# Where a residual block is turned: DMA transposes and TensorE transposes exchanged at two places, and joins written into spent space

## The chip, the cores and the metric

The kernel runs on one core of a Trainium2 chip. The metric is device time in microseconds (us), the median of several runs; less is better. The engines of the core are named as in the profile: PE is TensorE (PEld its weight loads), DVE is VectorE, ACT is ScalarE, POOL is GpSimd, SP is SyncE, which here only issues DMAs.

## The reference

One block of a hybrid streaming encoder, in float32, with 256 rows of 2048 columns. Cut to what matters here:

```python
h      = rmsnorm(x, g_mix);  proj = h @ w_in            # q,k,v twice, and two gates
merged = sigmoid(gate_sb) * (y_sb @ w_sb_out) + sigmoid(gate_ca) * (y_ca @ w_ca_out)
x      = x + merged @ w_mix_out
h      = rmsnorm(x, g_ffn);  g_ff, u_ff = split(h @ w_ffn_in)
x      = x + (silu(g_ff) * u_ff) @ w_ffn_out
h      = rmsnorm(x, g_ple)
x      = x + sigmoid(h @ w_ple_gate) * (p @ w_ple_in)   # the last gate
out    = rmsnorm(x, g_final)
```

`y_sb` is a stick-breaking attention and `y_ca` a chunked attention with a relative bias; neither is touched by the change.

## The kernel before

**Products.** Each float32 operand is split into a rounded high part and the remainder (`hi`, `lo`); a product is the sum of three TensorE products (`three`, L313). Activations lie in tables `T1`, `T2`, `T3`, transposed: a table holds, for each 128 columns of the activation (a `kt`, 16 of them for 2048 columns), a high and a low part of 128 x 256. A block is 512 columns, four `kt`. Weights are streamed from HBM in pieces of 128 x 1024 (`raw`, L244, issued on SP), cast on ACT (`hi`, L283, L298, L301) and subtracted on DVE (`lo`, L260). There are five `raw` buffers, one or two more in the later stages, and three or four pairs of `hi` and `lo`; casts run up to three pieces ahead of the products.

**Units.** Most products run in units of two blocks of output columns and all `kt`. In a unit some pairs of `kt` are pair pieces: seven products in place of eight, with sums of weights (`xf`, made on DVE and cast at L304) and sums of activations (`forms`, made by `sums_of` or `pair_sums`). The pair pieces add into four PSUM banks of their own (`su`), taken from the pool of banks that the unit before used for its results; `mid` (L883) copies them into the tile `C` (four planes of 128 x 512), and the unit's end adds `C` to the results. The mixer's two output projections (`w_sb_out`, `w_ca_out`) are not units: they are plain groups of four pieces for each block of 512 columns.

**Turning a block.** When a block of activations is ready, it must be transposed into a table. There are two ways.

`into_table` (L481) does eight 128 x 128 transposes on TensorE (L490) into PSUM; `table_part` then writes the high part on ACT and the low part on DVE from PSUM, times the gain of the norm where there is one (L543 and L544), and for `kt` whose pair is among `forms` it makes their sums.

`by_dma` (L497) takes the float32 words apart into 16-bit halves on ACT (`turn`, L506, two copies into `planes`), issues one DMA transpose of both planes on SP (L507, into `turned`), and later joins the halves again on ACT (`join`, L512, two copies of 128 x 1024 halves, one for each two `kt`) into a tile `af`, from which `table_part` goes on. The tag `af` has two buffers in the late stages; the joins, the squares of the norms (L125), `pair_sums` and the tile `fm` of `sums_of` all draw on it:

```python
af = state["work"]("af").rearrange("p (k s) -> p k s", k=2)
with tc.issue_after(state["cast"].ins):
    nc.scalar.copy(af.bitcast(U16).rearrange("p k (s h) -> p h k s", h=2), halves[:, :, k0 : k0 + 2, :])
table_part(dst, 4 * c + k0, af, gain, forms, pairs, af)
```

`at` gives how many pieces after the block the turn and the first join are put into the program; the second join follows one piece later.

**Who uses which.** `out_post` (L958) multiplies the mixer's projections by their gates, adds the two, and turns each of the four blocks (key `mg`, into `T1`) by `into_table`. `next_tables` (L1004) runs at the end of a unit for both of its blocks: after the mixer's last projection (key `ffn`, into `T3`) all four blocks go by DMA; after the last feed-forward projection (key `ple`, into `T1`) blocks 0 and 1 go by DMA and 2 and 3 by `into_table`. `hidden` (L1088) turns the feed-forward's hidden blocks, all but one by DMA.

**Order.** Work between pieces stands in two lists: `tasks`, one run after each piece (`later` puts three empty ones ahead), all of them before the first pair piece of a unit takes its banks; and `asides`, with the piece at which each is due. Within that, each engine's instructions are laid out by a planner, from a model of the timeline; `issue_after` holds an instruction behind another. SP issues the weight loads and the DMA transposes in one queue, in order.

Of the kernel before, what the change touches and what calls it, by code (L numbers as in the profile page):

```python
# [9 lines left out]
F32 = mybir.dt.float32  # L10
F32R = mybir.dt.float32r
U16 = mybir.dt.uint16
# [5 lines left out]
P = 128  # L18
S = 256
NT = 2  # L20
# [12 lines left out]
NB = 512  # L33
# [3 lines left out]
PAIRS = (2, 4, 6)  # L37
MIX_PAIRS = (4, 6)
# [15 lines left out]
def block_kernel(ctx: ExitStack, tc: tile.TileContext, x, p, w_in, w_sb_out, w_ca_out, w_mix_out,  # L54
# [19 lines left out]
    dma_w = nc.sync  # L74
# [12 lines left out]
    def aux(name):  # L87
        pool, width, tag = ps_ax[-1]
        return pool.tile([P, width], F32, tag=tag, name=name)
# [8 lines left out]
    T1 = bp.tile([P, KD, 2, S], F32R, tag="T1", name="T1")  # L98
    T2 = bp.tile([P, KD, 2, S], F32R, tag="T2", name="T2")
    x_ = bp.tile([P, NT, D], F32, tag="x", name="x")  # L100
# [306 lines left out]
    state = dict(loaded=0, split=0, at=0, raw=0, hl=0, ext=0, ps=ps_mm, fourth=None, ring=0, places=0, hold=False)  # L407
    late = dict(ps=[ps_mm])
# [27 lines left out]
    def later(fn, n=3):  # L436

        for _ in range(n):
            tasks.append((None, lambda: None))
        tasks.append((None, fn))  # L440
# [40 lines left out]
    def into_table(dst, c, src, gain=None, key=None, forms=None, pool=None, pairs=PAIRS):  # L481


        n = ps_ax[-1][1] // S if pool is None else 2
        for k0 in range(0, 4, n):
            ps = (aux("tp") if pool is None else late["ps"][pool].tile([P, 512], F32, tag="mm", name="tp"))
            ps = ps.rearrange("p (k s) -> p k s", k=n)
            for k in range(n):
                for t in range(NT):
                    nc.tensor.transpose(ps[:, k, t * P : (t + 1) * P], src[:, t, (k0 + k) * P : (k0 + k + 1) * P], ident)  # L490
            step = n if forms is None else 2
            for k1 in range(0, n, step):
                table_part(dst, 4 * c + k0 + k1, ps[:, k1 : k1 + step, :], gain, forms, pairs)
        for k in range(4):
            done.add((key, 4 * c + k))

    def by_dma(dst, c, src, planes, turned, key, at, gain=None, forms=None, pairs=PAIRS):  # L497

        words = src.bitcast(U16).rearrange("p t (k n h) -> p t h k n", h=2, n=P)
        planes, turned = (v.rearrange("p t n -> p (t n)").bitcast(U16) for v in (planes, turned))  # L500
        split = planes.rearrange("p (h k t n) -> p t h k n", h=2, k=4, t=NT)
        halves = turned.rearrange("p (h k s) -> p h k s", h=2, k=4)

        def turn():
            for t in range(NT):
                nc.scalar.copy(split[:, t], words[:, t])  # L506
            dma_w.dma_start_transpose(turned.rearrange("p (j s) -> p j s", s=P), planes)  # L507

        def join(k0):
            af = state["work"]("af").rearrange("p (k s) -> p k s", k=2)  # L510
            with tc.issue_after(state["cast"].ins):
                nc.scalar.copy(af.bitcast(U16).rearrange("p k (s h) -> p h k s", h=2), halves[:, :, k0 : k0 + 2, :])  # L512
            table_part(dst, 4 * c + k0, af, gain, forms, pairs, af)
            for k in range(k0, k0 + 2):
                done.add((key, 4 * c + k))

        turning.update((key, 4 * c + k) for k in range(4))
        asides.extend([(state["at"] + at[0], turn), *((state["at"] + at[1] + i, lambda i=i: join(2 * i)) for i in range(2))])
        asides.sort(key=lambda v: v[0])

    def table_part(dst, kt, ps, gain, forms, pairs, af=None):
        n = ps.shape[1]
        ks = slice(kt, kt + n)
        g = None if gain is None else [gT[:, gain + kt + k : gain + kt + k + 1] for k in range(n)]
        if forms is not None and kt // 2 in pairs:
            if af is None:
                af = state["work"]("af").rearrange("p (k s) -> p k s", k=2)
            if af is ps:
                pass
            elif g is None:  # L530
                nc.scalar.copy(af, ps)
            else:
                for k in range(2):
                    nc.scalar.activation(af[:, k, :], ps[:, k, :], AF.Identity, scale=g[k])
            nc.scalar.copy(dst[:, ks, 0, :], af)
            minus(dst[:, ks, 1, :], af, dst.bitcast(F32)[:, ks, 0, :])
            sums_of(af, forms(kt))
        elif g is None:
            nc.scalar.copy(dst[:, ks, 0, :], ps)
            minus(dst[:, ks, 1, :], ps, dst.bitcast(F32)[:, ks, 0, :])  # L540
        else:
            for k in range(n):
                nc.scalar.activation(dst[:, kt + k, 0, :], ps[:, k, :], AF.Identity, scale=g[k])  # L543
                nc.vector.scalar_tensor_tensor(dst[:, kt + k, 1, :], ps[:, k, :], g[k], dst.bitcast(F32)[:, kt + k, 0, :],  # L544
                                               ALU.mult, ALU.subtract)
# [375 lines left out]
    room = bp.tile([P, 4096], F32R, tag="x", name="room")  # L921
    later_y = T2.rearrange("p k c s -> p (k c s)")[:, KD * S :]
    F_gate = [FP[:, 0], FP[:, 1], *(t[:, 3072:].rearrange("p (c f s) -> p c f s", c=2, f=4) for t in (room, later_y))]
    work = mp.tile([P, 1024], F32, tag="v1", name="work")
# [25 lines left out]
    x_ = bp.tile([P, NT, D], F32, tag="x", name="x")  # L950
# [5 lines left out]
    work = mp.tile([P, 1024], F32, tag="v0", name="work")  # L956

    def out_post(m, c):  # L958
        def post(ps):
            cs = slice(c * NB, (c + 1) * NB)  # L960
            gt = gates[:, :, m, cs]
            for t in range(NT):
                by = rstd if (m, c) == (1, 0) else r1
                with tc.issue_after(state["cast"].ins):
                    nc.scalar.activation(gt[:, t, :], gt[:, t, :], AF.Sigmoid, scale=by["mix"][:, t : t + 1])
            for t in range(NT):
                nc.vector.tensor_tensor(gates[:, t, m, cs], ps[t], gates[:, t, m, cs], ALU.mult)
            if m == 1:
                mg = gates[:, :, 0, cs]
                nc.vector.tensor_tensor(mg, mg, gt, ALU.add)  # L970
                forms = lambda kt: FP[:, kt // 4 - 2]
                later(lambda: into_table(T1, c, mg, key="mg", forms=forms, pairs=MIX_PAIRS))
        return post

    for m, wo in ((0, w_sb_out), (1, w_ca_out)):
# [28 lines left out]
    def next_tables(T, c, gain, key, pool):  # L1004

        C = late["C"]
        room = late["pool"].tile([P, 2, NB], F32, tag="turned", name="turned")
        for cc in (c - 1, c):
            if key == "ffn" or cc < 2:
                planes, turned, at = (C[:, :2, :], room, (1, 5)) if cc < c else (C[:, 2:, :], C[:, :2, :], (3, 7))  # L1010
                by_dma(T, cc, x_[:, :, cc * NB : (cc + 1) * NB], planes, turned, key, at, gain)
                continue
            fn = lambda cc=cc: into_table(T, cc, x_[:, :, cc * NB : (cc + 1) * NB], gain, key, pool=pool)
            if cc == c:
                tasks.append((None, fn))
            else:
                later(fn)

    def mix_post(c0):
        def post(g, b):  # L1020
            c = c0 + b
            add_to_residual(g, b, c)
            if b == 1:
                next_tables(late["T3"], c, 16, "ffn", g["pool"])
            residual_done(c, "ffn")
            if c == 3:
                tasks.append(("p2", lambda: broadcast(p2bc, p2, late["pool"])))
        return post
# [59 lines left out]
    def hidden(dst, c, key, g, pairs):  # L1088
        C = late["C"]
        if key == "h0" and c == FF_BLOCKS[0] // 4 - 1:  # L1090
            later(lambda: into_table(dst, c, C[:, :2, :], key=key, pool=g["pool"], forms=out_form(pairs), pairs=pairs))
        else:
            by_dma(dst, c, C[:, :2, :], C[:, 2:, :], C[:, :2, :], key, (2, 6), forms=out_form(pairs), pairs=pairs)
# [40 lines left out]
    k0 = 0  # L1134
    for blk, nk in enumerate(FF_BLOCKS):
        key = f"h{blk}"
        for c in range(nk // 4):
            j = k0 // 4 + c
            unit(w_ffn_in[0], (j * NB, D_FF + j * NB), range(KD), T3, lambda kt: late["F"][0][kt // 4 - 1], rooms(T1),
                 C_slots, mid, (in_post if j else first_post)(T2, c, key, OUT_PAIRS[nk]), lambda kt: ("ffn", kt),  # L1140
                 pairs=PAIRS if j else (), after=None if j else scale_next)
# [124 lines left out]
```

## Time and profile before

| | |
|---|---|
| Time, median of 3 runs | 1453.84 us (1453.1 to 1454.06) |
| The profiled execution | 1452.93 us, its span 1451.2 us |
| PE busy | 1434.7 us, 99% of the span |
| DVE busy | 1248.7 us, 86% |
| ACT busy | 889.1 us, 61% |
| Weights and the rest by DMA | 299.55 MB, 206 GB/s mean |
| DMA transposes (L507) | 16, issue to landing 5.2 us median |
| Transposes for tables on TensorE (L490) | 56 |

A busy share is an average over the whole span. What a change in one stage is worth is read from that stage: how many matmuls TensorE does there, and on whom it waits. In a row of the timeline the first two numbers are the start and the length in us; in brackets stands how long the engine was idle before it and which instruction let it go. The granted clock (PEclk) is 1.00 at full speed.

### The profile page before, as it was taken

The numbers are of one execution on the slowest core, as the hardware profiler recorded it, in microseconds if no ns is written. First come the engines' busy times: TensorE is split into PE (matmuls) and PEld (weight loads), VectorE is DVE, ScalarE is ACT, GpSimd is POOL, SyncE is SP. The second block draws the span as 40 slices with busy tenths as digits, with TensorE's granted clock in tenths as the row PEclk, the third lists the DMA queues.
The fourth block names the chain that finished last, engine by engine and source line by source line (L and its number), as shares of the span: only waits on it lengthen the run. The fifth ranks groups of instructions, "written<-read, shape, count | busy, mean of one in ns | idle before, by whom it ended". The sixth has DMA issues, their size and how long they took to land.

```text
span 1451.2 us, 18508 instructions
## 1 busy us (share of the span) xinstructions
PE 1434.7 (99%) x6709; PEld 1195.6 (82%) x6709; DVE 1248.7 (86%) x1587; ACT 889.1 (61%) x1047; POOL 23.2 (2%) x44
## 2 busy tenths in 40 slices
PE   9999999999999999999999999999999999999997
PEld 7888888888888888888788888888887888887886
DVE  6979777888987767888999999999999999998775
ACT  6455556654545665587757656666755766778652
POOL 0200000000000000000000000000000000000000
PEclk9999999999999999999999999999999999999999
DMA  9866555566675555787666667676666676776871
GB/s 319 284 188 211 181 174 173 176 203 202 203 249 167 176 166 183 233 231 215 186 200 212 199 211 230 201 224 211 198 202 219 216 221 200 217 215 192 266 228 72
DMA packets 198011, 299.55 MB, mean 206 GB/s; under 512 B 42304, under 2 KB 75376, under 8 KB 197664
## 3 DMA queue, kind: packets, MB, share of 16 engines
q1 hardware_dynamic: 195808, 289.71, 64.6%
q0 software_dynamic: 2112, 8.68, 1.8%
q8 instruction: 52, 0.85, 0.2%
q14 instruction: 39, 0.32, 0.1%
HBM read 284.19 MB, written 5.77 MB: 200 GB/s over the span
## 4 chain that ended last, share of the span: by engine, by line
PE 93%; DVE 3%; ACT 2%; issue 1%; DMA 1%; SPq 0%; DVEq 0%; ACTq 0%
PE mm L313 66%; PE su L313 12%; PE mm L398 8%; PE mm L400 4%; DVE lo L260 1%; DMA raw<-in_w_in 1%; DMA raw<-in_w_ple_in 1%; ACT hi L283 1%; PE tp L490 0%; ACT af L512 0%; PE mml L313 0%; DVE xf L260 0%; PE xps L571 0%; ACT C L506 0%; DVE raw L260 0%
## 5 line engine op out<-in xcount | busy, mean ns | idle before, releaser
L313 PE MATMUL mm<-hi,T 128*128 128x512 f32 x2650 | 855.9, 391 | 3.3 <-ACT T L543 2.1
L260 DVE TENSOR_TENSOR lo<-raw,hi 128x1024 fp32r<-128x1024 f32 (+1 forms) x517 | 623.9, 1217 | 117.2 <-ACT hi L283 101.7
L283 ACT CAST hi<-raw 128x1024 fp32r<-128x1024 f32 (+1 forms) x379 | 395.8, 1049 | 318.4 <-PE mm L313 188.6
L313 PEld LDWEIGHTS mm<-hi,T 128*128 128x128 f32 x2650 | 498.1, 188 | 109.0 <-ACT T L543 2.5
L313 PE MATMUL mm<-lo,T 128*128 128x512 f32 x1325 | 517.3, 391 | 0.7 <-DVE lo L260 0.7
L313 PEld LDWEIGHTS mm<-lo,T 128*128 128x128 f32 x1325 | 249.3, 188 | 53.1 <-DVE lo L260 1.7
L398 PE MATMUL mm<-T,hi 128*128 128x512 f32 x512 | 179.8, 398 | 0.0
L400 PE MATMUL mm<-T,lo 128*128 128x256 f32 x512 | 139.5, 280 | 0.0
L301 ACT CAST hi<-raw 128x1024 fp32r<-128x1024 f32 x69 | 72.6, 1052 | 73.2 <-DVE raw L260 32.6
L260 DVE TENSOR_TENSOR T<-xf,T 128x1536 fp32r<-128x1536 f32 x61 | 106.9, 1753 | 10.4 <-ACT T L304 10.0
L398 PEld LDWEIGHTS mm<-T,hi 128*128 128x128 f32 x512 | 94.5, 188 | 20.2
L304 ACT CAST T<-xf 128x1536 fp32r<-128x1536 f32 x61 | 90.2, 1479 | 26.1 <-DVE xf L260 26.0
L260 DVE TENSOR_TENSOR xf<-raw 128x512 f32<-128x512 f32 x138 | 94.5, 685 | 10.8 <-DMA raw<-in_w_ffn_in 3.2
L400 PEld LDWEIGHTS mm<-T,lo 128*128 128x128 f32 x512 | 96.5, 189 | 2.3
L298 ACT CAST hi<-raw 128x1024 fp32r<-128x1024 f32 x69 | 72.4, 1050 | 28.9 <-PE mm L313 18.9
L313 PE MATMUL mm<-T,T 128*128 128x512 f32 (+1 forms) x279 | 77.5, 371 | 0.0
L313 PE MATMUL su<-hi,T 128*128 128x512 f32 x170 | 65.7, 391 | 0.2 <-ACT hi L298 0.2
L313 PEld LDWEIGHTS mm<-T,T 128*128 128x128 f32 x279 | 49.2, 188 | 9.1
L889 DVE TENSOR_TENSOR C<-su,C 128x512 f32<-128x512 f32 x72 | 47.6, 681 | 0.6 <-PE su L313 0.3
L313 PE MATMUL su<-T,FP 128*128 128x512 f32 x174 | 47.9, 389 | 0.0
L260 DVE TENSOR_TENSOR xf<-raw,xf 128x512 f32<-128x512 f32 x69 | 47.2, 685 | 0.6
L260 DVE TENSOR_TENSOR raw<-raw 128x512 f32<-128x512 f32 x69 | 47.2, 684 | 0.3
(287 smaller groups left out, 1275.7 us busy)
## 6 DMA issues: line engine op xcount, KB each, us to landing
raw<-in_w_ffn_in SPq DMA_DIRECT2D x176, 512.0 KB, 4.2
raw<-in_w_in SPq DMA_DIRECT2D x160, 512.0 KB, 4.1
raw<-in_w_ffn_out SPq DMA_DIRECT2D x88, 512.0 KB, 4.6
raw<-in_w_mix_out SPq DMA_DIRECT2D x32, 512.0 KB, 4.4
raw<-in_w_ple_gate SPq DMA_DIRECT2D x32, 512.0 KB, 5.1
raw<-in_w_sb_out SPq DMA_DIRECT2D x16, 512.0 KB, 3.8
raw<-in_w_ca_out SPq DMA_DIRECT2D x16, 512.0 KB, 4.5
x<-in_x SPq DMA_DIRECT2D x4, 512.0 KB, 10.5
```

The costliest lines, as they stand in the source:

```text
L260: return nc.vector.tensor_tensor(out, a, b, ALU.subtract)
L283: state["cast"] = nc.scalar.copy(hi[:, c : c + m], raw[:, c : c + m])
L298: nc.scalar.copy(h1, raw1)
L301: nc.scalar.copy(h2, raw2)
L304: nc.scalar.copy(xh, xf)
L313: state["mm"] = nc.tensor.matmul(ps, u, v, start=first, stop=last, skip_group_check=True)
L398: nc.tensor.matmul(ps, hi[:, i, f], lhs[:, kt, :, :].rearrange("p c s -> p (c s)"), start=a, stop=False)
L400: nc.tensor.matmul(ps[:, :S], lo[:, i, f], lhs[:, kt, 0, :], start=False, stop=z)
L889: nc.vector.tensor_tensor(C[i], q, C[j], ALU.add)
```

## The change

Three edits.

1. *Joins in the planes' space.* `join` writes its result over the planes, which the DMA transpose has read by then, in place of a new `af`. The first block of each pair in `next_tables` keeps `af` (`own`), since its planes are at the same time the other block's `turned`.
2. *Last gate's residual blocks by TensorE.* In `next_tables` the blocks 0 and 1 of the key `ple` go by `into_table`, as 2 and 3 did; the tile `turned` is taken for `ffn` alone.
3. *Three gated mixer outputs by DMA.* In `out_post` the blocks 0, 1 and 2 go by `by_dma`. Planes and results lie in the tile `gates`, where the two planes of a block are not adjacent, so each is turned by a DMA transpose of its own (`apart`). Block 3 stays with `into_table`.

```diff
-    def by_dma(dst, c, src, planes, turned, key, at, gain=None, forms=None, pairs=PAIRS):
+    def by_dma(dst, c, src, planes, turned, key, at, gain=None, forms=None, pairs=PAIRS, own=False, apart=False):
 
+        joined = planes
         words = src.bitcast(U16).rearrange("p t (k n h) -> p t h k n", h=2, n=P)
-        planes, turned = (v.rearrange("p t n -> p (t n)").bitcast(U16) for v in (planes, turned))
-        split = planes.rearrange("p (h k t n) -> p t h k n", h=2, k=4, t=NT)
-        halves = turned.rearrange("p (h k s) -> p h k s", h=2, k=4)
+        planes, turned = (v.bitcast(U16) for v in (planes, turned))
+        split = planes.rearrange("p h (k t n) -> p t h k n", k=4, t=NT)
+        halves = turned.rearrange("p h (k s) -> p h k s", k=4)
+        parts = [(turned[:, h], planes[:, h]) for h in range(2)]
+        if not apart:
+            parts = [[v.rearrange("p h n -> p (h n)") for v in (turned, planes)]]
 
         def turn():
             for t in range(NT):
                 nc.scalar.copy(split[:, t], words[:, t])
-            dma_w.dma_start_transpose(turned.rearrange("p (j s) -> p j s", s=P), planes)
+            for to, fro in parts:
+                dma_w.dma_start_transpose(to.rearrange("p (j s) -> p j s", s=P), fro)
 
         def join(k0):
-            af = state["work"]("af").rearrange("p (k s) -> p k s", k=2)
+            af = (state["work"]("af") if own else joined[:, k0 // 2, :]).rearrange("p (k s) -> p k s", k=2)
...
                 forms = lambda kt: FP[:, kt // 4 - 2]
-                later(lambda: into_table(T1, c, mg, key="mg", forms=forms, pairs=MIX_PAIRS))
+                if c < 3:
+                    by_dma(T1, c, mg, gt, mg, "mg", (2, 6), forms=forms, pairs=MIX_PAIRS, apart=True)
+                else:
+                    later(lambda: into_table(T1, c, mg, key="mg", forms=forms, pairs=MIX_PAIRS))
...
-        room = late["pool"].tile([P, 2, NB], F32, tag="turned", name="turned")
+        room = late["pool"].tile([P, 2, NB], F32, tag="turned", name="turned") if key == "ffn" else None
         for cc in (c - 1, c):
-            if key == "ffn" or cc < 2:
+            if key == "ffn":
                 planes, turned, at = (C[:, :2, :], room, (1, 5)) if cc < c else (C[:, 2:, :], C[:, :2, :], (3, 7))
-                by_dma(T, cc, x_[:, :, cc * NB : (cc + 1) * NB], planes, turned, key, at, gain)
+                by_dma(T, cc, x_[:, :, cc * NB : (cc + 1) * NB], planes, turned, key, at, gain, own=cc < c)
                 continue
```

## The prediction, made before the changed kernel was run

> **What bounds the kernel now.** I read the page first (span, busy shares, the chain that ended last), then the windows to find where TensorE does fewer matmuls than usual, then the timeline of those places.
>
> ```profile
> span 1451.2 us, 18508 instructions
> PE 1434.7 (99%) x6709; PEld 1195.6 (82%) x6709; DVE 1248.7 (86%) x1587; ACT 889.1 (61%) x1047; POOL 23.2 (2%) x44
> PE 93%; DVE 3%; ACT 2%; issue 1%; DMA 1%; SPq 0%; DVEq 0%; ACTq 0%
> ```
>
> TensorE (PE) is busy 99% and carries 93% of the chain. So a change can gain only by taking instructions off TensorE, or by closing the 16.5 us in which it is idle (1451.2 - 1434.7) and the slow stretch behind each gap. The windows show where these are; columns are busy time with the instruction count for each engine, then the granted clock.
>
> ```profile
> core 0: us, PE busy (x) PEld busy (x) DVE busy (x) ACT busy (x) POOL busy (x), PEclk, DMA share, GB/s
> 543.00:581.00 38.00, 38.00 (x186) 31.77 (x185) 28.03 (x35) 22.67 (x30) 0.00 (x0) 1.00 0.61 188
> 600.00:650.00 50.00, 50.00 (x222) 41.41 (x221) 45.67 (x55) 40.37 (x50) 0.00 (x0) 1.00 0.79 227
> 688.20:695.00 6.80, 4.70 (x14) 3.41 (x13) 5.84 (x11) 4.98 (x7) 0.00 (x0) 0.75 0.79 240
> 1312.00:1334.00 22.00, 20.68 (x88) 15.91 (x86) 19.80 (x26) 21.68 (x31) 0.00 (x0) 1.00 0.78 213
> 1320.00:1350.00 30.00, 27.32 (x106) 20.06 (x105) 26.16 (x32) 24.75 (x28) 0.58 (x1) 0.94 0.64 190
> ```
>
> The usual pace is 222 matmuls in 50 us, 0.225 us each. In the mixer's second projection (543 to 581) TensorE never rests. At the start of the first feed-forward unit (688.2 to 695) it does 14 matmuls where 30 would fit: 2.1 us idle, and a clock of 0.75 over 6.8 us, another 1.7 us; together 3.8 us lost (16 missing matmuls give 3.6). In the last output unit (1320 to 1350) it is idle 2.68 us and the clock of 0.94 costs 1.8 us, together 4.5; by count 27 of 133 matmuls are missing, 6.1 us. These two places and the transposes are what the change touches.
>
> First the feed-forward start:
>
> ```profile
> 667.02 3.16 SPq L507 DMA_TRANSPOSE C<-C  x1
> 687.14 0.28 DVE L260 TENSOR_TENSOR fm<-af,fm 128x128 f32<-128x128 f32 x1
> 687.98 1.34 ACT L512 COPY af<-C 128x1024 uint16<-128x1024 uint16 x1
> 690.13 0.90 ACT L543 ACTIVATE T<-af,gT 128x256 fp32r<-128x256 f32 x2
> 688.20 0.39 PE L313 MATMUL mm<-hi,T 128*128 128x512 f32 x1
> 690.69 0.50 PE L313 MATMUL mm<-hi,T 128*128 128x512 f32 x1 [2.10 <-ACT T L543]
> 691.41 0.63 PE L313 MATMUL mm<-hi,T 128*128 128x512 f32 x1
> ```
> ```profile
> DMA to landing us min/median/max: 3.9/5.2/6.7
> ```
>
> The last residual block's DMA transpose was issued at 667.02 and, by the landing row, was there by 673.7 at the latest. Its join (L512) ran only at 687.98, some 14 us later. What it waited for is its destination, `af`: that tag has two buffers, which the joins share with the squares of the norm, with `pair_sums` and with `fm`. The DVE row at 687.14 is the last reader of the `af` that `pair_sums` filled; 0.56 us after it ends the join starts. The table copy (L543) follows, and TensorE, which needs that table, stands still for 2.10 us and then runs matmuls of 0.63 us where 0.39 is usual.
>
> Then the last output unit:
>
> ```profile
> 1312.94 1.98 ACT L506 COPY C<-x 128x1024 uint16<-128x1024 uint16 x2
> 1317.02 1.98 ACT L506 COPY C<-x 128x1024 uint16<-128x1024 uint16 x2
> 1320.80 2.57 ACT L512 COPY af<-turned 128x1024 uint16<-128x1024 uint16 x2
> 1329.40 1.36 ACT L512 COPY af<-C 128x1024 uint16<-128x1024 uint16 x1 [0.25 <-DVE T L544]
> 1331.62 1.34 ACT L512 COPY af<-C 128x1024 uint16<-128x1024 uint16 x1
> 1333.80 1.03 ACT L301 CAST hi<-raw 128x1024 fp32r<-128x1024 f32 x1
> 1334.88 0.50 PE L313 MATMUL mm<-hi,F_more 128*128 128x512 f32 x1 [1.50 <-ACT hi L301]
> ```
>
> Here ScalarE (ACT) is full: 21.68 of 22 us. The weight cast (L301) that TensorE waits for stands behind 9.2 us of copies (1.98 + 1.98 + 2.57 + 1.36 + 1.34) that exist only because two residual blocks are turned by DMA.
>
> **The change part by part.** The prices:
>
> ```profile
> L490 PE MATMUL tp<-ident,gates 128*128 128x128 f32 x32 | 4.1, 272 | 0.0
> L490 PE MATMUL tp<-ident,x 128*128 128x128 f32 x16 | 2.1, 272 | 0.0
> L506 ACT COPY C<-x 128x1024 uint16<-128x1024 uint16 x12 | 11.9, 1037 | 0.0
> L512 ACT COPY af<-C 128x1024 uint16<-128x1024 uint16 x26 | 34.9, 1356 | 6.5 <-DMA C<-C 6.2 <-DVE T L544 0.3
> L507 SPq DMA_TRANSPOSE C<-C x13: 1401/3109/4591, 625.1 to 1319.4; - x13
> L531 ACT COPY work<-tp 128x512 f32<-128x512 f32 x2 | 1.2, 586 | 0.3 <-PE tp L490 0.3
> 502.99 46.41 SPq L244 DMA_DIRECT2D raw<-in_w_ca_out  x16
> ```
>
> *Mixer, three of four blocks by DMA.* Removed from TensorE: 3 x 8 transposes; 32 take 4.1 us, so 8 take 1.03 and 24 take 3.1. TensorE is full there, so all of it lies on the path: -3.1. Added on ACT, for each block: two copies of 1.04 and two joins of 1.36, 4.8 us; one copy of 0.59 (L531) goes in the third block. All three make 14.4 - 0.6 = 13.8, of which the third block's joins (2.7) fall after 581, since a join comes six and seven pieces after its block and a piece takes 12 x 0.225 = 2.7 us. So ACT goes from 22.67 to about 33.8 of 38 us: full at 89%, and I cost it at nothing, covered by the casts that now wait for TensorE. Without that cover each delayed cast costs what the one at 1334.88 did (rival B). Deadlines: by the order of the pieces each block is used five or six pieces after its joins (the first ends with piece 4, is joined after 10 and 11 and used from 17 on), 13 us; the third has its sums on DVE to make within that. On SP two half-size transposes for each block go in among loads that come one in 2.9 us (46.41 / 16). A whole transpose holds SP 3.1 us (1.4 to 4.6), two halves somewhere between that and twice it, 9.2, plus the wait for the copies. The weight loads behind them find five buffers of 2.7 us, 13.5 us, less the landing. I take 0; the ends are 0 and, if that cover is gone, one stall like that at 1334.88 for each block (1.5 + 1.8 = 3.3).
>
> The Trainium skill, page "VectorE: DVE Perf Modes", section "The three transpose paths", puts a 128x128 bf16 transpose at 390 ns on TensorE and 1309 ns by DMA, and its rules send it to TensorE wherever PSUM will do as destination. By that this part gains nothing, the sum would lack its 3.1 and be -4.9, 1448.9. The rows here set another price: 1.03 us of the engine that bounds against 5.2 us of landing beside it.
>
> *Last gate's blocks 0 and 1 by TensorE.* Added: 16 transposes, which took 2.1 us for blocks 2 and 3: +2.1. Removed: the 9.2 us on ACT above, two DMA transposes and their waits on SP. The scaled table copies (L543, L544) stay, reading PSUM. So ACT falls from 21.7 to 12.5 of 22 us and the cast at 1333.80 can run up to 9 us sooner. Late next is DVE: 26.16 of 30 us busy, so this stretch cannot shrink by more than 3.8. The stall is 4.5 to 6.1 long; what it can give back lies between 0 and 6.1, and DVE's room is the nearest row: I take 4.0 gross, 1.9 net of the transposes.
>
> *Joins in the planes' space.* Nothing is added; the join of the later block of each unit no longer waits for `af`. At the feed-forward start that join may run at 674, so the whole 3.8 us may go. Late next is DVE once more:
>
> ```profile
> 702.29 2.35 DVE L260 TENSOR_TENSOR lo<-raw,hi 128x1024 fp32r<-128x1024 f32 x2
> 704.20 0.39 PE L313 MATMUL mm<-lo,T 128*128 128x512 f32 x1
> ```
>
> The first of these two remainders is ready near 703.5 and used at 704.20, 0.7 us of room. If TensorE comes 3.8 us sooner, DVE (5.84 of 6.80 busy) must put them ahead of other work. Between 0 and 3.8 I take 3.0. `C` is now held until the table copies have read it, eight or nine pieces after the unit; its next writer, `mid` of the next unit, comes behind ten, so I cost this at nothing; without that cover ACT's copy of the sums would wait a piece, 2.7 us, of ScalarE's time. In the other feed-forward units TensorE has no gap after joins: nothing.
>
> The Trainium skill, page "TensorE: Matmul & The Clock Gate", section "HAM oscillation — how this bites in real kernels", lets the clock fall only after an idle gap above some 3.4 us. By that the two gaps would cost their idle time alone, 2.1 and 2.7, and the sum with all of it given back would be -3.1 + 2.1 - 2.7 - 2.1 = -5.8. The trace disagrees: after 2.10 us the matmuls take 0.63 us and the window's clock is 0.75.
>
> *Sum:* -3.1 + 2.1 - 4.0 - 3.0 = -8.0 us. The profiled execution took 1452.93 us (span 1451.2), so 1444.9; the median of the runs, 1453.84, lies 0.9 above it: **1445.8**. With everything given back it is -3.1 + 2.1 - 6.1 - 3.8 = -10.9, 1442.9.
>
> **Rivals.** A measurement of this kernel can tell about 0.2%, 2.9 us, from no change: faster ends at 1450.9, slower begins at 1456.7.
>
> *A. DVE takes the place of both waits.* For: it is busy 19.80 of 22 and 5.84 of 6.80 us where the gains should be. Against: it is not full there, and in the first place its work is only reordered. Then only the transposes count, -1.0, with about one more: 1451.9, no change.
>
> *B. ScalarE becomes the bound in the mixer.* Place: 543 to 581, at 89% by my count. Price: a weight cast behind two copies or two joins, 3.3 us each time TensorE waits as at 1334.88; there are six such bursts. From three (9.9 against -8.0) the gain is gone; at four it is +5.2, 1459.0, slower. For: in 1312 to 1334 a full ACT did this. Against: there it was at 99%, and 600 to 650 shows 40.37 of 50 with no gap.
>
> *C. The sums' PSUM banks come late.* The two blocks now pass through the four banks that the first pair of the last output unit needs.
>
> ```profile
> L544 DVE SCALAR_TENSOR_TENSOR T<-tp,gT,T x8: 472/474/479, 1363.9 to 1368.2; 128x256 fp32r<-128x256 f32 x8
> 798.27 0.39 PE L490 MATMUL tp<-ident,C 128*128 128x128 f32 x2
> 805.41 0.68 DVE L260 TENSOR_TENSOR T<-af,T 128x512 fp32r<-128x512 f32 x1
> 1314.26 0.39 PE L313 MATMUL mm<-T,T 128*128 128x512 f32 x1
> ```
>
> One block held its banks 7.8 us (798.27 to 806.1). Two, from about 1314.5, may hold them 11.6 (3.8 more, eight table writes of 0.47 on DVE), while TensorE has three pieces, 36 x 0.225 = 8.1 us, that need no such bank: 3.5 idle and 1.8 of clock, -8.0 + 5.3, 1451.1. It decides when the hold passes 8.1 us. Against: ACT and DVE get there early once the copies are gone.
>
> **How the numbers follow.** Forecast 0.65, A 0.15, B 0.13 (0.08 of it slower, the rest no change), C 0.07 (0.02 slower). With A's and C's fringes: faster 0.67, no change 0.22, slower 0.11. The forecast's own range is 1442.5 to 1449.5; to hold 8 in 10 it must take in A and C and the mild half of B, up to 1455. Left out are the slower cases and a few per cent below 1442.5.
>
> **What would show it.** Right: L490 has 8 transposes from `gates` and 32 from `x`; the join at the feed-forward start runs within some 3 us of its DMA's landing and the 2.10 gap before L313 is gone; ACT from 1312 to 1334 is well below full and no gap of 1.5 us stands before a weight cast's user; TensorE stays full from 543 to 581. Wrong: gaps released by `lo` on DVE at those places (A), gaps released by a cast in the mixer (B), `su` matmuls that wait for L544 (C), or casts there that wait for loads behind L507 on SP. The engines' orders are laid out by a planner from a model of the timeline; if it puts the earlier join or the table copies behind other work all the same, the gaps stay and A's time holds.

## The result and the profile after

The changed kernel took 1463.53 us (median of 4 runs, 1462.17 to 1465.65) against 1453.47 for the kernel before on the same chip: a ratio of 1.0073, 95% interval 1.0057 to 1.0089. It is slower by about 10 us, where 8 less were forecast. The profiled execution took 1462.17 us. Lines of its page:

```profile
span 1460.4 us, 18511 instructions
PE 1439.1 (99%) x6701; PEld 1190.3 (82%) x6701; DVE 1248.5 (85%) x1587; ACT 889.7 (61%) x1050; POOL 23.3 (2%) x44
PE 32%; DVE 5%; DMA 3%; issue 2%; ACT 1%; DVEq 0%; ACTq 0%
```

Eight TensorE instructions fewer (6701 against 6709), the same work on DVE and ACT, and a span 9.2 us longer. The chain, 93% TensorE before, now spends 8% on DVE and DMA. (It accounts for 43% of the span only, so I use it no further.) The stretches shown before, and two inside the feed-forward:

```profile
core 0: us, PE busy (x) PEld busy (x) DVE busy (x) ACT busy (x) POOL busy (x), PEclk, DMA share, GB/s
543.00:581.00 38.00, 38.00 (x174) 31.53 (x173) 28.45 (x34) 32.43 (x39) 0.00 (x0) 1.00 0.83 240
688.20:695.00 6.80, 6.80 (x32) 5.63 (x31) 6.80 (x10) 2.63 (x3) 0.00 (x0) 1.00 0.70 233
1000.00:1050.00 50.00, 49.03 (x211) 38.93 (x211) 46.85 (x58) 33.90 (x39) 0.00 (x0) 1.00 0.67 200
1250.00:1300.00 50.00, 47.48 (x203) 36.87 (x201) 45.33 (x59) 36.12 (x41) 0.00 (x0) 1.00 0.69 210
1320.00:1350.00 30.00, 29.21 (x131) 22.31 (x130) 28.31 (x36) 18.74 (x28) 0.00 (x0) 1.00 0.51 170
```

The two feed-forward stretches in the kernel before:

```profile
1000.00:1050.00 50.00, 50.00 (x223) 41.39 (x222) 47.45 (x61) 35.95 (x40) 0.00 (x0) 1.00 0.66 196
1250.00:1300.00 50.00, 50.00 (x222) 41.27 (x221) 46.87 (x59) 35.40 (x40) 0.00 (x0) 1.00 0.68 197
```

The places that the prediction spoke of behave as it said: 32 matmuls where 14 stood (688 to 695), 131 where 106 stood (1320 to 1350), no gap in the mixer's projection. The loss is where it said "nothing": 12 and 19 matmuls are missing in two stretches of the feed-forward in which TensorE had no gap.

To place gains and losses I counted, for each kernel, the `three` matmuls (L313) done from the start to a time t (windows from 0 to t, that line alone), and took off the count of the kernel before. One matmul is 0.225 us; plus is ahead.

| kernel | 580 | 600 | 688 | 720 | 850 | 1300 | 1400 |
|---|---|---|---|---|---|---|---|
| the change | +14 | -1 | -4 | +14 | -2 | -41 | -40 |
| joins alone (e1) | -1 | -1 | -1 | +17 | -14 | -31 | -36 |
| gate alone (e2) | -1 | -1 | -2 | 0 | 0 | -6 | +7 |
| mixer alone (e3) | +13 | -10 | -18 | -29 | -31 | -51 | -53 |
| change, hidden joins in `af` (e4) | +13 | -9 | -11 | +7 | -5 | -26 | -13 |
| joins alone, hidden ones apart (e8) | +3 | +4 | +3 | +21 | +7 | +8 | +17 |
| joins and gate, hidden ones apart (e9) | +5 | +5 | +4 | +22 | +4 | +5 | +24 |
| the change, hidden ones apart (e10) | +13 | -9 | -11 | +7 | -8 | -5 | +7 |
| e9 without turning mixer blocks (e13) | +15 | +15 | +14 | +33 | +25 | +25 | +34 |
| e10 without the mixer's DMA transposes (e14) | +13 | -8 | -10 | +8 | -7 | -10 | +1 |
| e10 with two mixer blocks (e16) | +12 | +10 | +9 | +27 | +8 | +6 | +18 |
| gate and the residual joins (e5) | -2 | -6 | -8 | +11 | -1 | -5 | +8 |
| e1, hidden joins in a tile of their own (e6) | +3 | +3 | +2 | +20 | -8 | -23 | -28 |
| e4, fourth mixer block earlier (e7) | +8 | -28 | -31 | -12 | -17 | -39 | -26 |
| e10, two `raw` buffers later (e11) | +15 | -1 | -2 | +17 | +2 | -3 | +9 |
| before, hidden joins apart (e12) | +2 | 0 | -1 | +1 | +1 | -2 | -2 |
| e10, mixer's turns earlier (e15) | +4 | -38 | -57 | -40 | -49 | -58 | -50 |

Each row is one profiled run. The seven kernels that leave the mixer as it was (e1, e2, e5, e6, e8, e9, e12) stand between -6 and +5 at 600, so a difference of a few matmuls says nothing. The last column times 0.225 gives the change +9.0 us, its span says +9.2. The change is ahead by 14 after the mixer and loses it within 20 us; gains 18 at the feed-forward start and loses 16 of them by 850; then loses 39, 8.8 us, from 850 to 1300. TensorE idles 4.5 us of those 450 us, where it idled 0.3 before; where the rest of the 39 went was not followed. The kernels e1 to e16 follow.

### The profile page after: what moved, and what is told of

Same layout as the page of the kernel before. It is cut to its first block, busy times and chain, and to the rows that moved or that the text cites. A ratio compares the mean times of both kernels' runs of the same rounds, so it can differ in the third digit from the quotient of the medians.

```text
span 1460.4 us, 18511 instructions
## 1 busy us (share of the span) xinstructions
PE 1439.1 (99%) x6701; PEld 1190.3 (82%) x6701; DVE 1248.5 (85%) x1587; ACT 889.7 (61%) x1050; POOL 23.3 (2%) x44
## 5 line engine op out<-in xcount | busy, mean ns | idle before, releaser
L313 PE MATMUL mm<-hi,T 128*128 128x512 f32 x2650 | 855.1, 391 | 5.2 <-ACT hi L283 2.8
L313 PEld LDWEIGHTS mm<-hi,T 128*128 128x128 f32 x2650 | 496.8, 188 | 114.7 <-ACT hi L283 7.8
L313 PE MATMUL mm<-lo,T 128*128 128x512 f32 x1325 | 516.5, 390 | 2.0 <-DVE lo L260 1.9
L313 PEld LDWEIGHTS mm<-lo,T 128*128 128x128 f32 x1325 | 248.7, 188 | 56.6 <-DVE lo L260 5.3
L260 DVE TENSOR_TENSOR T<-xf,T 128x1536 fp32r<-128x1536 f32 x61 | 106.8, 1752 | 10.8 <-ACT T L304 10.5
L313 PE MATMUL mm<-T,T 128*128 128x512 f32 (+1 forms) x279 | 77.6, 371 | 0.0
L313 PE MATMUL su<-hi,T 128*128 128x512 f32 x170 | 66.1, 392 | 0.2 <-DVE T L549 0.2
L313 PEld LDWEIGHTS mm<-T,T 128*128 128x128 f32 x279 | 49.3, 188 | 9.1
L894 DVE TENSOR_TENSOR C<-su,C 128x512 f32<-128x512 f32 x72 | 47.7, 682 | 2.2 <-PE su L313 1.8
L313 PE MATMUL su<-T,FP 128*128 128x512 f32 x174 | 48.3, 391 | 0.0
```

Source lines behind the costliest of these rows:

```text
L260: return nc.vector.tensor_tensor(out, a, b, ALU.subtract)
L313: state["mm"] = nc.tensor.matmul(ps, u, v, start=first, stop=last, skip_group_check=True)
L894: nc.vector.tensor_tensor(C[i], q, C[j], ALU.add)
```

## The experiments

All ratios are to runs of the kernel before on the same chip. Diffs are against the changed kernel, with - for what it has, unless another is named. The letters of theories are those of the expectations; they are not the prediction's rivals.

**Which edit costs.** Theory J: the joins of the hidden blocks, side by side on ACT, are the cost. Rival G: the gate or the mixer.

e1, the joins' edit alone:
```diff
-                if c < 3:
-                    by_dma(T1, c, mg, gt, mg, "mg", ...)
-                else:
-                    later(lambda: into_table(T1, c, mg, ...))
+                later(lambda: into_table(T1, c, mg, ...))
...
-            if key == "ffn":                  # in next_tables
+            if key == "ffn" or cc < 2:
```


> Edit 1 alone: joins in the planes' space; the mixer's blocks and the last gate's blocks are turned as before. Theory J (the joins lose: without the wait for af both joins of a block stand side by side right behind the DMA transpose, so ScalarE waits for the DMA and the casts behind it come late): the feed-forward start gains 3 to 4 us and the feed-forward units lose 8 to 12, so 1457 to 1463 us, with more than 15 us of ScalarE time idle before joins for their DMA (18.8 in the changed kernel, 6.2 before). Theory G (the loss is the last gate's or the mixer's doing): 1449 to 1451.

e2, the gate's edit alone: the mixer as in e1, and `own=True` (join into `af`) in every call of `by_dma`.

> Edit 2 alone: the last gate's residual blocks 0 and 1 by TensorE, all joins into af, mixer as before. Theory J: as the prediction had this part by itself, 2 us faster, 1450 to 1453. Theory G: slower by 3 us or more.

e3, the mixer's edit alone: the gate's blocks 0 and 1 by DMA again, `own=True` in every call.

> Edit 3 alone: three mixer blocks by two DMA transposes each, joined into the work tile, the rest as before. The prediction had -3.1 for it. In the changed kernel's trace the 3.1 us of transposes are gone but a gap near 592 us eats them. Theory J: no change, 1452 to 1455. Theory G: slower by 3 us or more, with a gap above 2 us near 590.

e4, the change with the hidden blocks' joins in `af`:
```diff
-     key, (2, 6), forms=out_form(pairs), pairs=pairs)
+     key, (2, 6), forms=out_form(pairs), pairs=pairs, own=True)
```


> The changed kernel with the joins of the feed-forward's hidden blocks back in af (the mixer's and the residual's joins stay in the planes' space). Theory J: the feed-forward's loss is gone and the gain at its start is kept, 1447 to 1451. Theory G: still 1459 or more.

Measured: e1 1.005 (1.0035 to 1.0064), e2 0.9988 (0.9978 to 0.9998), e3 1.0083 (1.0064 to 1.0101), e4 1.0014 (1.0004 to 1.0023). The joins' edit alone loses 7 us, and sending only the hidden joins back to `af` takes the change from 1.0073 to 1.0014 (1455.92 us, where J asked for 1447 to 1451). J holds for most of the loss, but G is right about the mixer, which alone loses 12: of e3's matmuls 23 go from 580 to 600, 11 at the feed-forward start, whose wait for `af` it keeps, and 20 from 850 to 1300. The gate gains 1.7.

What the hidden joins do is seen in the timeline of one block. Before, with `af`:

```profile
1285.56 1.35 ACT L512 COPY af<-C 128x1024 uint16<-128x1024 uint16 x1 [1.13 <-DMA C<-C]
1288.66 1.05 ACT L283 CAST hi<-raw 128x1024 fp32r<-128x1024 f32 x1
1291.09 1.36 ACT L512 COPY af<-C 128x1024 uint16<-128x1024 uint16 x1
```

After, with the join in the planes' space (L517 is the join, L512 before; the DVE rows of `fm` are sums of activations; the bracket is the idle time before the row and what ended it):

```profile
1292.09 2.56 ACT L517 COPY C<-C 128x1024 uint16<-128x1024 uint16 x2 [3.24 <-DMA C<-C]
1293.48 0.29 DVE L474 TENSOR_TENSOR fm<-C 128x128 f32<-128x128 f32 x1 [2.38 <-ACT C L517]
1294.53 1.03 ACT L283 CAST hi<-raw 128x1024 fp32r<-128x1024 f32 x1
1295.59 1.23 DVE L260 TENSOR_TENSOR lo<-raw,hi 128x1024 fp32r<-128x1024 f32 x1 [1.41 <-ACT hi L283]
1295.61 0.49 PE L313 MATMUL mm<-hi,T 128*128 128x512 f32 x1 [1.03 <-ACT hi L283]
1296.87 0.50 PE L313 MATMUL mm<-lo,T 128*128 128x512 f32 x1 [0.76 <-DVE lo L260]
```

With the two buffers of `af` the second join came 5.5 us after the first, and casts of weights ran between. Without them both joins are one stretch of 2.56 us, behind a wait of 3.24 us for the DMA transpose. ACT works in order, so the cast that TensorE needs stands behind 5.8 us of waiting and joining; DVE, 45 of 50 us busy here, idles 2.38 and 1.41 us, and TensorE stands twice. Over the whole span (waits: us, times, longest):

```profile
ACT C L517 <- DMA C<-C: 18.8, 9, 3.2
DVE fm L474 <- ACT C L517: 13.0, 10, 2.7
```

Before, what ended ACT's idle time before a join, and who waited for it:

```profile
  DMA C<-C: 6.2, 7
  DVE fm L474: 3.6, 3
```

e1 has only 10.8 us of that wait, less than its expectation asked for, and e4, whose joins are 5.5 us apart, still has 14.6. So there may be two costs here, the wait and the joins side by side; the next runs part them.

**Is it `C` that is held longer, or the joins side by side?** e5 keeps edit 2 and the residual joins of the feed-forward start alone; e6 is e1 with the hidden joins in a tile of their own, so that `C` comes free early (H: that `C` held longer is the cost); e7 is e4 with the mixer's fourth block two pieces earlier; e8 is e1 with the second hidden join one piece later still.

```diff
+   joined = late["pool"].tile([P, 2, NB], F32, tag="turned", name="joined")   # e6, hidden blocks, in turn()
...
-   later(lambda: into_table(T1, c, mg, ...))        # e7, block 3
+   later(lambda: into_table(T1, c, mg, ...), n=1)
...
-   (state["at"] + at[1] + i, lambda i=i: join(2 * i))     # e8, hidden blocks
+   (state["at"] + at[1] + 2 * i, lambda i=i: join(2 * i))
```


> Edit 2, and of edit 1 only the residual's joins after the mixer's last projection; hidden blocks into af, mixer by TensorE. Compared with e2_gate (1451.4) it adds only the shorter wait at the feed-forward start. Theory K (the gain is kept): the 2.1 us gap near 690 is gone, 16 matmuls more by 720 us than before, and still about 16 more at 1300: 1447 to 1449. Theory D (the vector engine, near full behind that place, cannot follow, and gives the gain back): 16 more by 720, less than 5 more by 850, 1450.5 to 1452.5.

> As e1_joins (1460.9), but the hidden blocks' joins go into a tile of their own (turned, unused in those units) in place of the planes: no wait for af and C is given back as early as before. Theory J (both joins side by side on ScalarE, waiting for the DMA, are the cost): no different from e1_joins, 1458 to 1463. Theory H (C held until the table copies have read it is the cost): back to 1449 to 1453.

> As e4_ffn_af (1455.9), but the mixer's fourth block, still turned by TensorE, is put in two pieces earlier (one empty task ahead of it, not three). Theory M (a load of w_mix_out into memory that the mixer frees waits for the fourth block's sums on VectorE, and TensorE for that load): the gap of 1.9 us near 594 and its slow stretch go, 1449 to 1453, and at 600 us some 10 matmuls more than e4. Theory S (the DMA transposes' places on SP, or their traffic, hold the load up): no change, 1455 to 1457.

> As e1_joins (1460.9), but the second join of a hidden block comes two pieces after the first, not one, so casts stand between them. C is held longer still. Theory J: most of the 8 us come back, 1450 to 1455. Theory H: no better than e1_joins, 1460 or more.

Measured: e5 0.9975 (0.9965 to 0.9984), e6 1.0037 (1.0024 to 1.0049), e7 1.0028 (1.0017 to 1.004), e8 0.9964 (0.9951 to 0.9976). e6 is as slow as e1 within the intervals, and e8, which holds `C` longer still, recovers all of e1's loss: H falls, J stands. e5 took 1449.6 us, between the ranges of K (the gain at the start is kept) and D (DVE gives it back); its matmuls speak for D, since of 19 gained from 688 to 720 it has 7 left at 850. In e8's trace a cast runs between the joins again:

```profile
1280.49 1.36 ACT L517 COPY C<-C 128x1024 uint16<-128x1024 uint16 x1 [0.53 <-DMA C<-C]
1283.61 1.05 ACT L283 CAST hi<-raw 128x1024 fp32r<-128x1024 f32 x1
1284.56 1.35 ACT L517 COPY C<-C 128x1024 uint16<-128x1024 uint16 x1
```

With ACT's wait for these transposes beside the matmuls lost from 850 to 1300, the two costs seem to part. Joins apart: e8 waits 5.9 us and loses none (it gains 1), e2 waits 7.2 and loses 6; e5 and e9 to e16, described below, wait 5.3 to 11.0 us and lose at most 9. Joins apart but long waits: e4 14.6 us and 21, e3 23.5 and 20, e7 18.8 and 22. Side by side with short waits: e6 8.2 us and 15, e1 10.8 and 17. Both: the change, 18.8 us and 39. Each alone goes with some 15 to 22 matmuls (3.4 to 5.0 us), both with 39. By edits: the joins alone lose 17 (e1), the mixer alone 20 (e3), the change 39, and the whole change with its joins apart none (e10, with a wait of 9.6 us). (From 720 to 850 the pattern is less clean: e1 and e6 lose 31 and 28, the change and e8 16 and 14.) What lengthens the wait was not tried by itself. In the one instance that I followed, near 940 to 950 us, SP issued the transpose 0.5 us behind a weight load in e3 and 1.7 us behind one in the kernel before, and it took 5.1 us to land against 3.9; that the place among the loads is the cause is argued, not shown.

**With the joins apart, what are the other edits worth?** e9 is edits 1 and 2 so spaced, e10 the whole change so spaced, e11 is e10 with the two extra `raw` buffers taken into use six pieces later, e12 is the kernel before with the same spacing.

```diff
-    more_places(lambda: lp.tile([P, 1024], F32, tag="raw", ...), MORE)     # e11
+    state["more"] = lambda: lp.tile([P, 1024], F32, tag="raw", ...)
+    asides.append((state["at"] + 6, lambda: state.update(places=MORE)))
```


> Edits 1 and 2 with the second join of a hidden block two pieces after the first; mixer by TensorE as before. e8_apart gave 0.9964 of the kernel before and edit 2 alone 0.9988; if the two are apart in time and do not touch each other: 0.995, some 7 us faster. If the vector engine is the bound by now, no better than e8_apart.

> The whole change with the second join of a hidden block two pieces after the first. Theory J (joins side by side) and theory M (the mixer's 3 us are lost again at the hand-over of memory near 590): some 10 us better than the change, 2 to 4 us worse than e9_gate_apart, about 1449 to 1452. If the mixer's part is harmless once the joins stand apart: as e9_gate_apart or up to 3 us better.

> As e10_all_apart, but the two extra raw buffers, which lie in memory that the mixer frees, are taken into use six pieces later. Theory M: the load that waited 5 us for VectorE's FP is gone, with it the gap near 594, and the mixer's 3 us are kept: 3 to 6 us better than e10_all_apart. Theory S (the DMA transposes' traffic and places on SP): no better, or worse for want of the two buffers.

> The kernel before, joins in af as they were, with the second join of a hidden block two pieces after the first. Theory J: the wait for af stood between the joins already in most units, so little changes: within 2 us of before. If the spacing is a gain by itself, whatever the place of the joins: 4 us or more faster.

Measured: e9 0.9968 (0.9955 to 0.998), e10 0.9982 (0.9973 to 0.999), e11 0.9985 (0.9976 to 0.9993), e12 1.0001 (0.9992 to 1.001). Spacing does nothing while `af` spaces the joins anyway (e12). e9 missed its expectation: in time the gate adds nothing measurable to e8, whose gate stretch gained 9 matmuls without that edit (1300 to 1400: +8 to +17). In its trace e9 gains 19 there, but that is the fastest of its five runs. And the mixer's edit still gains nothing: e10 is 13 matmuls ahead at 580, 9 behind at 600. e11 missed the 3 to 6 us of theory M.

**Where the mixer's gain goes.** After the change, at 585 to 594:

```profile
585.44 0.62 ACT L478 CAST FP<-work 128x512 fp32r<-128x512 f32 x1 [2.16 <-DVE work L260]
586.09 0.69 DVE L260 TENSOR_TENSOR FP<-work,FP 128x512 fp32r<-128x512 f32 x1 [0.69 <-ACT FP L478]
593.56 0.50 PE L313 MATMUL mm<-hi,FP 128*128 128x512 f32 x1 [1.77 <-ACT hi L301]
```

In the waits of SP's queue of loads the fourth block's sums (`FP`) are the longest of this stretch, a load of `w_mix_out` into memory that the mixer hands over:

```profile
SPq L244 <- DVE FP L260: 5.1, 1, 5.1
```

The weights behind the gap come later too. DVE takes up the first of them, let go by the load, at 590.97 in the changed kernel and at 589.48 in e9:

```profile
590.97 0.69 DVE L260 TENSOR_TENSOR xf<-raw 128x512 f32<-128x512 f32 x1 [1.80 <-DMA raw<-in_w_mix_out]
```
```profile
589.48 0.69 DVE L260 TENSOR_TENSOR xf<-raw 128x512 f32<-128x512 f32 x1 [2.23 <-DMA raw<-in_w_mix_out]
```

e7 had the last sum 2.3 us sooner than e4 (584.05 against 586.31), but SP's wait for it grew to 6.9 us and TensorE stood 6.03 us behind a weight cast (28 matmuls behind at 600): it tells nothing of that wait alone. e11 took the wait away, and smaller gaps came in its place, 0.51 and 0.60 us behind remainders on DVE and 0.95 us behind a cast that waited for another load; it still loses 16 matmuls from 580 to 600, where e10 loses 22. So I left work out:

e13 is e9 without any turning of the mixer's blocks 0 to 2 (24 transposes; the expectation's 48 is a slip); e14 is e10 without the mixer's six DMA transposes, its joins reading the planes as they are. In both, three blocks go on unturned.
```diff
-                for t in range(NT):           # e13, into_table
+                for t in range(0 if key == "mg" and c < 3 else NT):
                     nc.tensor.transpose(...)
...
-            for to, fro in parts:             # e14, turn
+            for to, fro in ([] if key == "mg" else parts):
                 dma_w.dma_start_transpose(...)
```


> Gate edit and joins in the planes' space with the joins spaced, and the mixer's blocks 0 to 2 not turned at all: their 48 small TensorE transposes are left out and nothing takes their place (no transpose by DMA, no copy before it, no join behind it); the copy that followed the transposes reads the block as it stands. This leaves out the turning of three of the four mixer blocks, so its time is a bound for any way of turning them off TensorE. Three theories of why the same kernel with DMA transposes (1451.29 us, ratio 0.9982) is no faster than the one with TensorE transposes (1450.12, ratio 0.9968), though TensorE is 8 matmuls ahead at 580 us: W (the loads of w_mix_out bind from 585 us on: they go into memory that VectorE hands back, and TensorE arrives at weights that have not come): the head start of about 12 matmuls over the TensorE version at 580 is there, and by 600 it is lost again in gaps of TensorE of 2 us or more, count at 600 and at 688 within 5 of that version, time 1449 to 1452, ratio 0.996 to 0.9985. A (the copies and joins on ScalarE delay the fourth block's sums): the head start stays through 600 and 688, at least 10 matmuls, time about 1447.5, ratio 0.995. S (the DMA transposes hold the queue of loads or the DMA engines): the same as A here.

> The whole change with the joins spaced, without the mixer's six DMA transposes alone: the copies into planes and the joins on ScalarE stay, and the joins read the planes as they are, so three mixer blocks go on unturned. W: head start of 13 matmuls at 580 over the kernel before as with the DMA transposes, lost by 600; time as with them, 1450 to 1452.5. A: the same, lost at 600, since the copies and joins are still there; time 1450 to 1452. S: the head start stays through 600 and 688, time about 1447.5, ratio 0.995. So with the other run: lost in both is W, kept in the other and lost here is A, kept in both is S.

Measured: e13 0.9942 (0.9929 to 0.9954), 15 matmuls ahead at 580 and still 15 at 600; e14 0.9987 (0.9978 to 0.9996), 13 ahead, then 8 behind. So the loads do not bind by themselves (W falls as put: with the same head start, and the sums 5 us sooner, they come in time), the DMA transposes at this place are free (S falls), and the loss comes from ACT's copies and joins (A). The fourth block's last sum, in e9, e13 and e14:

```profile
583.32 0.69 DVE L260 TENSOR_TENSOR FP<-work,FP 128x512 fp32r<-128x512 f32 x1
```
```profile
578.18 0.68 DVE L260 TENSOR_TENSOR FP<-work,FP 128x512 fp32r<-128x512 f32 x1
```
```profile
586.41 0.69 DVE L260 TENSOR_TENSOR FP<-work,FP 128x512 fp32r<-128x512 f32 x1 [0.69 <-ACT FP L478]
593.82 0.50 PE L313 MATMUL mm<-hi,FP 128*128 128x512 f32 x1 [1.68 <-ACT hi L301]
```

With the edit TensorE comes 1.8 us sooner than in e9 (8 matmuls at 580) and the sums that hand the memory over come 3.1 us later (586.41 against 583.32); the gaps that follow cost e14 21 matmuls. Is it the joins' place (P) or ACT's load (L)? e15 issues turns and joins earlier; e16 leaves block 2 to TensorE. Both against e10:

```diff
-   by_dma(T1, c, mg, gt, mg, "mg", (2, 6), ...)
+   by_dma(T1, c, mg, gt, mg, "mg", (1, 4), ...)     # e15
...
-                if c < 3:
+                if c < 2:                            # e16
```


> The whole change with the hidden units' joins spaced, and the mixer's turns and joins issued earlier: the turn one piece after its block instead of two, the joins four and five pieces after it instead of six and seven. Without turning at all the head start of TensorE stayed (1445.19 us, ratio 0.9942), and without the DMA transposes alone it was lost as before (1451.47, 0.9987); so it is the copies and joins on ScalarE. Two theories of how. P (their place: the third block's joins, at 574.9 and 577.5 us, stand just ahead of the fourth block's copies and push its sums on VectorE from 583.3 to 586.5): the third block's joins come at about 571 to 574, the fourth block's last sum by about 584, the head start of about 8 matmuls over the TensorE version stays at 600, time 1446.5 to 1448.5, ratio 0.995 to 0.9965. L (the added time of ScalarE, 32.4 us of work in 543 to 581 against 22.1 with TensorE transposes, wherever it stands): the stall at 590 to 594 stays above 1 us, time 1450 to 1452.5, ratio 0.998 to 0.9995. A wait of ScalarE on the DMA transposes (they land about 5.7 us after the turn) could take what P gives; then the time lies between.

> The whole change with the hidden units' joins spaced, and in the mixer only blocks 0 and 1 turned by DMA; blocks 2 and 3 by TensorE. 16 transposes of 0.13 us leave TensorE instead of 24: a head start of about 9 matmuls at 580 over the TensorE version at most. P: block 2's copies are where the TensorE version has them (its sum 566 to 574), so the fourth block's sums come at about 583 or a little earlier, no stall near 590: head start of 5 to 9 matmuls kept through 600, time 1447.5 to 1449, ratio 0.9955 to 0.9965. L: ScalarE carries two thirds of the added work, so the stall is there at two thirds, about 1 to 1.5 us, and the time is 1449.5 to 1451.5, ratio 0.9975 to 0.999.

Measured: e15 1.0077 (1.0064 to 1.0091), far off both theories: the joins came before their transposes had landed, and ACT with all its casts stood still.

```profile
582.80 1.33 ACT L517 COPY gates<-gates 128x1024 uint16<-128x1024 uint16 x1 [5.60 <-DMA gates<-gates]
584.16 0.29 DVE L474 TENSOR_TENSOR work<-gates 128x128 f32<-128x128 f32 x1 [5.70 <-ACT gates L517]
```

TensorE was 38 matmuls behind at 600. So e15 doesn't part P from L; it shows that the joins cannot come that early. e16 took 0.9969 (0.9958 to 0.9981): 12 matmuls ahead at 580, 10 at 600, its last `FP` sum at 582.13 and no gap above 0.1 us in 590 to 595:

```profile
582.13 0.69 DVE L260 TENSOR_TENSOR FP<-work,FP 128x512 fp32r<-128x512 f32 x1
```

That is P's trace, where L asked for a stall of 1 to 1.5 us. A load of ACT that hurts only with the third block is not excluded. The ratio lies just above P's range and cannot be told from e9's. The 5 matmuls that it is ahead of e9 at 600 are 6 behind by 1400.

## Why the prediction was wrong, point by point

**The step that failed: "In the other feed-forward units TensorE has no gap after joins: nothing."** That stretch measured 39 matmuls, 8.8 us, from 850 to 1300: the largest term, and about half of the way from the forecast's -8 to the measured +10. The missing gap was read as freedom, but it was `af` that kept the joins apart; the question to ask there was which order ACT takes when that wait goes. I had asked "what is late next" at the feed-forward start only. The joins' edit alone loses 17 there (e1) and the mixer's edit alone 20 (e3). That the mixer's edit reaches so far was no term of the sum; its kernels have the longer waits for DMA transposes, and why stays open. The rest of the way is, in the change, the mixer (4 behind at 688, 4.0 us short of its -3.1), the feed-forward start (2.6 us) and the gate (1.7 us). The cost that I did name for this edit, `C` held longer, is nothing, as forecast (e6, e8).

**Mixer, -3.1.** The price was right: 14 matmuls ahead at 580 are 3.15 us, and e13 keeps 15. ACT's 33.8 us by my count were 32.43, and no gap came from 543 to 581, so rival B did not happen as put. But the cost of 0 on ACT failed: the gain was lost right behind the window that I looked at, between 580 and 600. The deadline "the third has its sums on DVE to make within that" was the right one to look at, and I followed it for the third block alone: by e16 its joins push back the fourth block's sums, which hand memory to the load queue. The cost of 0 was 3.4 us in the change (15 matmuls from 580 to 600); e10 stands 14 matmuls behind e9 at 600.

**Feed-forward start, -3.0 of at most 3.8.** The join runs 4.2 us after its transpose was issued (672.73), the 2.10 gap is gone and the clock is full:

```profile
676.93 2.57 ACT L517 COPY C<-C 128x1024 uint16<-128x1024 uint16 x2
688.04 0.62 PE L313 MATMUL mm<-hi,T 128*128 128x512 f32 x2
```

From 688 to 720 it gained 18 matmuls, 4.1 us, a little more than all of it. But it is given back further on: by 850 e8 has 4 of its 18 left, e9 none, e5 7 of 19. Kept, it is 0 to 1.6 us (e13 keeps 11, 2.5 us). In e8 TensorE stands there twice, 1.03 us near 784 and 1.14 us near 818, for ACT's copies of `x` into PSUM banks (L354); before the first ACT itself waited for DVE to take the sums out of the banks (L894):

```profile
783.47 0.59 ACT L354 COPY mm<-x 128x512 f32<-128x512 f32 x1 [4.40 <-DVE C L894]
784.11 0.50 PE L313 MATMUL mm<-hi,T 128*128 128x512 f32 x1 [1.03 <-ACT mm L354]
```

So DVE is late next, as the prediction had it, but by the banks and some 80 us further on than it looked, since its sum stopped at 704. Whether DVE alone is behind the second wait was not shown.

**Gate, -1.9.** e2 gave 0.9988, -1.7 us, and in its trace 13 matmuls from 1300 to 1400 (2.9 us). The stall of 1.50 is gone, the transposes cost what was said, and ACT is at 18.74 of 30 us where it had 24.75:

```profile
L490 PE MATMUL tp<-ident,x 128*128 128x128 f32 x32 | 4.3, 272 | 0.0
```

Rival C (`su` matmuls that wait for L544, now L549) showed a wait of 0.23 us in the changed kernel, and one of 1.1 us in e10, e11 and e13 to e16, where 3.5 were feared. In the whole change the stretch from 1300 to 1400 gave 1 matmul net.

**Rival A** (DVE in place of the waits) was true in part of what the feed-forward start gave back, and of nothing else that the runs show. The slower side, 0.11 in my chances, had a mechanism on ACT as its bearer (B), on the right engine and in the wrong stage.

The Trainium skill, page "VectorE: DVE Perf Modes", section "Rules for kernel authors", would send transposes to TensorE wherever PSUM will do as the destination. The runs agree for three blocks of the mixer, though not by the durations of the transposes: the DMA transposes cost nothing there (e14, 0.9987, as slow as e10, 0.9982), while the copies and joins around them on ACT cost some 6.5 us (e14 against e13, 0.9942), more than the 3.1 us of TensorE that they free.

## What to carry to other kernels

A wait for a buffer may be what spaces an engine's work: before it is taken away, ask what the engine does next in its order, and put the spacing back by hand; here one piece more between two copies turned +0.5% into -0.4%. In this kernel a transpose by DMA is paid on the engine that takes its words apart and joins them, and whatever stands behind a join there waits for the landing (up to 5.60 us in e15). A gain on the bounding engine is worth only what the next buffer hand-over lets it keep, so follow it past the window in which it is made. The fastest whole kernels are e8 (0.9964), e9 (0.9968) and e16 (0.9969), which cannot be told apart: joins in the planes' space with the hidden ones apart; the gate and two mixer blocks add nothing that these runs can measure. Nor can they be told from e5 (0.9975), whose hidden joins stay in `af`: what the spaced hidden joins are worth by themselves is not shown.

## What was not expected of the hardware

The clock. After a gap of 1.68 us, e14's matmuls run at 0.63 us for some 3 us; after one of 1.77 us in the changed kernel, at the same place, they run at 0.39 to 0.40:

```profile
595.88 0.63 PE L313 MATMUL mm<-hi,FP 128*128 128x512 f32 x1
```
```profile
593.89 0.40 PE L313 MATMUL su<-hi,FP 128*128 128x512 f32 x1
```

So the length of one gap does not decide it, and these runs do not show what does. It is also what puts e10, with the same mixer edit, 8 matmuls behind the change at 600: from 595 to 600 TensorE did 15 matmuls in e10 and 23 in the change. The Trainium skill, page "TensorE: Matmul & The Clock Gate", section "HAM oscillation — how this bites in real kernels", gives as its rule that no idle gap should exceed some 3.4 us. By that figure the clock should have stayed; in e14 and in e10 (1.81 us, granted clock 0.70 from 595 to 600) it fell all the same, as after 2.10 us before the change.
